# Weight tiles loaded through GpSimd's queue in a four-mixer encoder trunk

## The chip, the core and the metric

The kernel runs on one core of a Trainium2 chip. Its engines each have an instruction stream of their own: PE (TensorE, the matmuls), DVE (VectorE), ACT (ScalarE), POOL (GpSimd) and SP (SyncE). Transfers between HBM and the on-chip memory are issued by SP, ACT or POOL, each in the order of its stream. The metric is the device time in microseconds (us); less is better.

## The reference

Input is `x`, 1 × 512 × 1024 in float32, and the model has two layers. Each layer is a hybrid block of four parallel mixers, then a feed-forward part:

```python
h = RMSNorm(x)
P = h @ W_in          # columns shared out among four mixers and four gates
A: Mamba-2 SSD        B: sparse attention with top-k keys ("dsa")
C: RWKV-7             D: S5 diagonal state space model per 16-channel group
m = sum_n sigmoid(gate_n(h)) * (y_n @ W_branch_n);  x = x + m @ W_out
x = x + SwiGLU(RMSNorm(x))
```

A final RMSNorm follows the second layer. All is float32.

## The kernel before

**Projections.** Activations stand transposed: 1024 features are 8 blocks of 128 partitions, 512 tokens are the free dimension. Every weight matrix is cut into tiles of 128 output columns (`raw`: 128 partitions × 8 blocks × 128 columns, 512 KB). A float32 product is made of three matmuls in a faster format: weights are split into a high part `wh` and a rest `wl`, activations into `hh` and `hl`, and `mm3` (lines 299 to 301) does wh·hh, wh·hl and wl·hh. With 8 blocks a tile takes 24 matmuls of 128 × 512.

**The weight pipeline** is `wload` (line 282): a transfer fills `raw` (line 291, `RAW` = 2 buffers), ACT casts it to `wh` (line 292, 2 buffers), DVE subtracts to give `wl` (line 293, 2 buffers). There are 336 weight tiles in 338 transfers (two tiles come in two pieces). A buffer of `raw` is free when the subtraction of its tile has ended.

**The mixers.** In each layer come S5 (in two halves of 16 groups), dsa, RWKV (two halves) and SSD. Their small operations have long chains on DVE and ACT; projections for the gates (`fill`) stand between them so that PE has work. After them come the merge of the branches, the output projection and the feed-forward, dense series of weight tiles. During the feed-forward of layer 0, the S5 tables of layer 1 are made ahead and put by in HBM.

In the S5 half (`s5`), `s5kt` and `s5pt` are small matmuls on a table `s5E` made by DVE; a result goes to HBM (`ktd`) and comes back as eight pieces into `s5T` (line 1010), over a memset (line 1008). `s5px` is the first matmul series of the half, its result goes twice through a swap of partition halves by transfers (`s5xs`, lines 1004 and 1005) with DVE work between, and `s5py` (lines 1028 and 1029) needs `s5T` and the end of that chain.

At the start, `xtp` (line 218) are transposes of the input, `rbp` (line 185) is a matmul on two small loads, `oh` and `rb`, that prepares the attention's bias, and `colp` (line 442) transposes parameter columns.

**The order.** A scheduler sets each engine's order from priorities (`at("w")` gives weight loads the highest but one) and from times that it estimates. So a change of one operation's engine also moves others.

**Queues.** `q(c)` picks the issuing engine of a transfer by its class from `QUEUE`; a class that isn't there goes to SP. POOL (`"p"`) has the S5 parameters (`sp`, into `s5raw`), `ktd` and `s5T` (`kt`), and the attention's `bias` (`bi`, 8 a layer); some POOL transfers are written out (`oh`, `rb`, `rel`, `dsk`, `dsq`, the S5 tables' way to HBM and back). POOL also does memsets: `mask` (line 617), `s5T`, `NZ` (line 1193, RWKV) and `sdS` (line 1411, SSD).

Of the kernel before, what the change touches and what calls it, by code (L numbers as in the profile page):

```python
# [61 lines left out]
RAW = 2  # L62
FILL = (22, 4, 6)
AH = (2, 8, 11)
QUEUE = {"sp": "p", "qk": "a", "lc": "a", "sv": "a", "kt": "p", "bi": "p"}
FSLOT = ["A0", "A1", "A2", "A3"]
HSLOT = ["A0", "A1", "A2", "A3", "A4", "A5", "B0", "B1", "B2", "B3", "B4"]

# [17 lines left out]
class Trunk:  # L86
# [15 lines left out]
    def q(self, c):  # L102
        return {"a": self.nc.scalar, "p": self.nc.gpsimd, "s": self.nc.sync}[QUEUE.get(c, "s")]

# [177 lines left out]
    def wload(self, pieces, KT, M):  # L282
        nc = self.nc
        n = KT * M
        with self.at("w"):
            raw = self.wp.tile([128, 1024], F32, name="raw", bufs=RAW)
            wh = self.wp.tile([128, 1024], F32R, name="wh")
            wl = self.wp.tile([128, 1024], F32R, name="wl")
            r3 = raw[:, :n].rearrange("p (k m) -> p k m", m=M)
            for m0, src in pieces:  # L290
                nc.sync.dma_start(r3[:, :, m0:m0 + src.shape[1]], src.rearrange("(k p) m -> p k m", p=128))
            nc.scalar.copy(wh[:, :n], raw[:, :n])  # L292
            nc.vector.tensor_sub(wl[:, :n], raw[:, :n], wh[:, :n].bitcast(F32))  # L293
        f = lambda t: t[:, :n].rearrange("p (k m) -> p k m", m=M)
        return f(wh), f(wl)
# [1215 lines left out]
```

## Time and profile before

| what | value |
|---|---|
| time, median of 3 runs | 2346.5 us (2345.83 to 2346.74) |
| time of the profiled execution | 2347.53 us |
| its span, first to last instruction | 2345.7 us |
| PE busy | 2284.1 us, 97% |
| DVE busy | 1435.8 us, 61% |
| ACT busy | 902.8 us, 38% |
| POOL busy | 103.6 us, 4% |
| mean granted clock of PE | 0.988 of full speed |

The profiled execution's time is the span and 1.8 us around it. An engine's busy time leaves out the instructions that issue transfers, so POOL's 4% has no issues in it. The granted clock is 1.00 at 2.4 GHz and 0.50 at 1.2 GHz.

### The profile page before, as it was taken

What the parts mean: (1) busy time and instruction counts of PE and PEld (TensorE: products, weight loads), DVE (VectorE), ACT (ScalarE), POOL (GpSimd) and SP (SyncE); (2) the same over time, 40 slices, a digit from 0 to 9 for tenths busy, and PEclk for the clock granted to TensorE, in tenths of its full rate; (3) what the DMA queues carried; (4) which work ended last, traced back from release to release, by engine and by line L of the source; (5) the groups of instructions that cost most, each with busy time, mean ns of one, the idle gap of its engine ahead of it and who ended that gap; (6) DMA issues with size and microseconds to landing.
All of it is one profiled execution on the core that took longest, in us unless ns stands there. A gap on an engine that the chain in (4) does not pass through costs nothing.

```text
span 2345.7 us, 31925 instructions
## 1 busy us (share of the span) xinstructions
PE 2284.1 (97%) x12348; PEld 1829.7 (78%) x12348; DVE 1435.8 (61%) x2680; ACT 902.8 (38%) x1455; POOL 103.6 (4%) x180
## 2 busy tenths in 40 slices
PE   6999999999999999999999999999999999999998
PEld 5787767877778888887878777677777888888786
DVE  6669767856678597543343695668566775444433
ACT  5343454333552343322232335533346333222223
POOL 3320000000000101000011000000000000000000
PEclk9999999999999999999998999999999999999999
DMA  7545453334166435433365554434242653333232
GB/s 217 123 116 156 123 170 88 108 94 130 37 205 213 118 90 164 129 99 104 117 182 139 131 153 136 134 94 114 76 126 95 207 171 91 99 99 99 86 99 86
DMA packets 421679, 294.17 MB, mean 125 GB/s; under 512 B 56624, under 2 KB 378240, under 8 KB 419928
## 3 DMA queue, kind: packets, MB, share of 16 engines
q1 hardware_dynamic: 412016, 265.58, 38.9%
q0 software_dynamic: 8512, 26.43, 4.1%
q8 instruction: 97, 1.59, 0.3%
q14 instruction: 54, 0.44, 0.1%
q10 hardware_dynamic: 1000, 0.13, 0.0%
HBM read 237.27 MB, written 51.40 MB: 123 GB/s over the span
## 4 chain that ended last, share of the span: by engine, by line
PE 87%; DVE 8%; DMA 2%; issue 2%; ACT 1%; SPq 0%; DVEq 0%; ACTq 0%
PE pj L300 17%; PE pj L301 17%; PE pj L299 17%; PE pf L301 3%; PE pf L300 3%; PE pf L299 3%; PE pb L300 3%; PE pb L301 3%; PE pb L299 3%; DVE wl L293 2%; PE ptp L671 1%; PE lgp L653 1%; PE rwP L1253 1%; PE rwA L1174 1%; PE po L676 1%
## 5 line engine op out<-in xcount | busy, mean ns | idle before, releaser
L299 PE MATMUL pj<-hh,wh 128*128 128x512 f32 x1888 | 751.1, 398 | 5.8 <-DVE conv L1365 2.0
L300 PE MATMUL pj<-hl,wh 128*128 128x512 f32 x1888 | 750.7, 398 | 0.1
L301 PE MATMUL pj<-hh,wl 128*128 128x512 f32 x1888 | 747.3, 396 | 0.9 <-DVE wl L293 0.9
L292 ACT CAST wh<-raw 128x1024 fp32r<-128x1024 f32 x336 | 348.8, 1038 | 946.9 <-PE pj L300 378.0
L293 DVE TENSOR_TENSOR wl<-raw,wh 128x1024 fp32r<-128x1024 f32 x336 | 405.1, 1206 | 373.9 <-ACT wh L292 372.9
L299 PEld LDWEIGHTS pj<-hh,wh 128*128 128x128 f32 x1888 | 356.4, 189 | 89.9 <-issue 9.1
L300 PEld LDWEIGHTS pj<-hl,wh 128*128 128x128 f32 x1888 | 356.3, 189 | 79.6 <-issue 5.8
L301 PEld LDWEIGHTS pj<-hh,wl 128*128 128x128 f32 x1888 | 356.1, 189 | 79.5 <-issue 3.9
L299 PE MATMUL pf<-hid,wh 128*128 128x512 f32 x352 | 137.9, 392 | 1.6 <-ACT wh L292 1.6
L301 PE MATMUL pf<-hid,wl 128*128 128x512 f32 x352 | 137.7, 392 | 0.5 <-DVE wl L293 0.5
L300 PE MATMUL pf<-hid,wh 128*128 128x512 f32 x352 | 137.0, 390 | 0.0
L301 PE MATMUL pb<-yh,wl 128*128 128x512 f32 x256 | 101.1, 395 | 0.0
L300 PE MATMUL pb<-yl,wh 128*128 128x512 f32 x256 | 101.1, 395 | 0.0
L299 PE MATMUL pb<-yh,wh 128*128 128x512 f32 x256 | 100.6, 393 | 0.0
L533 DVE TENSOR_TENSOR fa<-fa,pj 128x512 f32<-128x512 f32 x44 | 30.2, 687 | 95.1 <-PE pj L301 95.0
L530 DVE TENSOR_TENSOR fa<-pj,rb 128x512 f32<-128x512 f32 x44 | 30.4, 690 | 88.5 <-PE pj L301 88.5
L299 PEld LDWEIGHTS pf<-hid,wh 128*128 128x128 f32 x352 | 66.1, 188 | 16.9 <-ACT wh L292 3.4
L301 PEld LDWEIGHTS pf<-hid,wl 128*128 128x128 f32 x352 | 66.1, 188 | 15.9 <-DVE wl L293 2.6
L300 PEld LDWEIGHTS pf<-hid,wh 128*128 128x128 f32 x352 | 66.1, 188 | 13.5
L661 ACT ACTIVATE lg<-lg,mn 128x128 f32<-128x128 f32 (+3 forms) x64 | 35.8, 559 | 62.4 <-DVE mn L659 56.0
L658 DVE TENSOR_TENSOR lg<-lgp,bias 128x128 f32<-128x128 f32 (+3 forms) x64 | 30.8, 486 | 43.1 <-PE lgp L653 42.9
L301 PEld LDWEIGHTS pb<-yh,wl 128*128 128x128 f32 x256 | 48.1, 188 | 10.8 <-issue 0.8
(481 smaller groups left out, 3051.1 us busy)
## 6 DMA issues: line engine op xcount, KB each, us to landing
raw<-in_w_in SPq DMA_DIRECT2D x146, 512.0 KB
raw<-in_ffn_w SPq DMA_DIRECT2D x120, 512.0 KB
gates<-gate SPq DMA_DIRECT2D x64, 256.0 KB
gld<-gates SPq DMA_DIRECT2D x64, 256.0 KB
raw<-in_w_branch SPq DMA_DIRECT2D x32, 512.0 KB
raw<-in_w_out SPq DMA_DIRECT2D x16, 512.0 KB
raw<-in_ffn_w SPq DMA_DIRECT2D x16, 384.0 KB
s5xs<-s5UX SPq DMA_DIRECT2D x16, 256.0 KB
```

The lines of the kernel that those rows point to most:

```text
L292: nc.scalar.copy(wh[:, :n], raw[:, :n])
L293: nc.vector.tensor_sub(wl[:, :n], raw[:, :n], wh[:, :n].bitcast(F32))
L299: mm(ps, wh, ah, start=first, stop=False)
L300: mm(ps, wh, al, start=False, stop=False)
L301: mm(ps, wl, ah, start=False, stop=last)
L530: nc.vector.tensor_mul(a, p1, rb)
L533: nc.vector.tensor_mul(a, a, p3)
L653: i = mm(ps[e][:, :W], q[er[e], qt * 128:(qt + 1) * 128], k[er[e], :W], start=True, stop=True)
L658: nc.vector.tensor_add(t[:, :W], ps[e][:, :W], bias[e][:, 384 - 128 * qt:512])
L661: nc.scalar.activation(t[:, :W], t[:, :W], AF.Exp, scale=-1.0, bias=mn[e][:, qt:qt + 1], accum_out=sm[e][:, qt:qt + 1])
L671: nc.tensor.transpose(pp[:, b * 128:(b + 1) * 128], t[:, b * 128:(b + 1) * 128], self.ident)
L676: i = mm(po[er[e], qt * 128:(qt + 1) * 128], vt[:, b, er[e]], pt[:, e, b * 128:(b + 1) * 128], start=(b == 0), stop=(b == qt))
```

## The change

Weight transfers get a class `"w"`, which `QUEUE` sends to POOL:

```diff
-QUEUE = {"sp": "p", "qk": "a", "lc": "a", "sv": "a", "kt": "p", "bi": "p"}
+QUEUE = {"sp": "p", "qk": "a", "lc": "a", "sv": "a", "kt": "p", "bi": "p", "w": "p"}
...
             for m0, src in pieces:
-                nc.sync.dma_start(r3[:, :, m0:m0 + src.shape[1]], src.rearrange("(k p) m -> p k m", p=128))
+                self.q("w").dma_start(r3[:, :, m0:m0 + src.shape[1]], src.rearrange("(k p) m -> p k m", p=128))
```

All 338 transfers move from SP's stream to POOL's. In the dense series PE, ACT and DVE keep their order; among the mixers and at the start the scheduler orders them anew.

POOL's stream at the start, before, from the last S5 parameter on (`oh`, `rb`, `rel`: loads and stores for the attention's bias; `sm`: a constant):

```order
L761 DMA s5raw<-in_s_c_im 128x4x64
L181 DMA oh<-in_onehot 32x512
L182 DMA oh_224<-in_onehot 32x128
L183 DMA rb<-in_rel_bias 32x8
L173 MEMSET sm_99 128x512
L174 MEMSET sm_99 128x8
L617 MEMSET mask 128x128
L618 MEMSET mask 64x64
L191 DMA rel<-oh 8x512
```

The same place after the change:

```order
L761 DMA s5raw<-in_s_c_im 128x4x64
L291 DMA raw<-in_w_in 128x8x128 x2
L617 MEMSET mask 128x128
L181 DMA oh<-in_onehot 32x512
L618 MEMSET mask 64x64
L182 DMA oh_224<-in_onehot 32x128
L183 DMA rb<-in_rel_bias 32x8
L173 MEMSET sm_99 128x512
L174 MEMSET sm_99 128x8
L291 DMA raw<-in_w_in 128x8x128 x2
```

The first two weight loads come in ahead, and `mask` has moved in front of the loads `oh` and `rb`.

PE's stream at the start, before, from the last transposes of the input to `rbp` (`pj` is the sum of the first weight tile):

```order
L218 MATMUL xtp<-cst,xsB_108 128x128
L299 MATMUL pj<-hh,wh 128x512
L300 MATMUL pj<-hl,wh 128x512
L301 MATMUL pj<-hh,wl 128x512
L299 MATMUL pj<-hh,wh 128x512
L185 MATMUL rbp<-oh,rb 8x512
L187 MATMUL rbp_231<-oh_224,rb 8x128
L300 MATMUL pj<-hl,wh 128x512
```

And after; here these are the first weight matmuls of the program, while before three rows of this kind stand further up between the transposes:

```order
L218 MATMUL xtp<-cst,xsB_108 128x128
L299 MATMUL pj<-hh,wh 128x512
L300 MATMUL pj<-hl,wh 128x512
L299 MATMUL pj<-hh,wh 128x512
L300 MATMUL pj<-hl,wh 128x512
L185 MATMUL rbp<-oh,rb 8x512
L187 MATMUL rbp_231<-oh_224,rb 8x128
L228 MATMUL xrp<-cst,xin_79 128x128
```

Fewer weight matmuls stand ahead of `rbp`, and those with `wl` have moved behind it.

POOL's stream in the first S5 half of layer 0, after the change (the pieces of `s5T`; before, the eight stand in a row with nothing between):

```order
L1010 DMA s5T<-ktd 16x2048
L291 DMA raw<-in_w_in 128x8x128
L1010 DMA s5T<-ktd 16x16x112
L291 DMA raw<-in_w_in 128x8x128
L1010 DMA s5T<-ktd 16x16x96
L291 DMA raw<-in_w_in 128x8x128
L1010 DMA s5T<-ktd 16x16x80
L291 DMA raw<-in_w_in 128x8x128
L1010 DMA s5T<-ktd 16x16x64
L291 DMA raw<-in_w_in 128x8x128
L1010 DMA s5T<-ktd 16x16x48
L1010 DMA s5T<-ktd 16x16x32
```

Five weight loads have come between the pieces; the last three pieces stand behind the fifth.

## Rows read from the trace of the kernel before

**Rows 1.** Page: the span and the busy time of each engine.

```profile
span 2345.7 us, 31925 instructions
PE 2284.1 (97%) x12348; PEld 1829.7 (78%) x12348; DVE 1435.8 (61%) x2680; ACT 902.8 (38%) x1455; POOL 103.6 (4%) x180
```

**Rows 2.** Timeline, steady feed-forward: start, duration, engine, line, operation, [idle before, releaser].

```profile
1022.05 1.06 ACT L292 CAST wh<-raw 128x1024 fp32r<-128x1024 f32 x1 [3.87 <-issue]
...
1027.49 1.05 ACT L292 CAST wh<-raw 128x1024 fp32r<-128x1024 f32 x1 [3.86 <-issue]
...
1023.14 1.23 DVE L293 TENSOR_TENSOR wl<-raw,wh 128x1024 fp32r<-128x1024 f32 x1 [0.21 <-ACT wh L292]
...
1024.39 5.80 SPq L291 DMA_DIRECT2D raw<-in_ffn_w  x2
```

**Rows 3.** Windows: length, PE, PEld, DVE, ACT, POOL busy, PEclk, DMA share, GB/s.

```profile
1027.00:1027.50 0.50, 0.50 (x4) 0.40 (x3) 0.00 (x0) 0.01 (x1) 0.00 (x0) 1.00 0.97 293
1027.50:1028.00 0.50, 0.50 (x4) 0.42 (x3) 0.33 (x1) 0.50 (x1) 0.00 (x0) 1.00 0.11 31
```

**Rows 4.** Transfers: issuing queue, count, KB each, median us from issue to landing.

```profile
raw<-in_ffn_w SPq DMA_DIRECT2D x120, 512.0 KB
...
raw<-in_w_branch SPq DMA_DIRECT2D x32, 512.0 KB
raw<-in_w_out SPq DMA_DIRECT2D x16, 512.0 KB
raw<-in_ffn_w SPq DMA_DIRECT2D x16, 384.0 KB
...
bias<-relb POOLq DMA_DIRECT2D x16, 256.0 KB, 3.4
...
s5raw<-in_s_b_im POOLq DMA_DIRECT2D x4, 128.0 KB, 7.5
...
s5T<-ktd POOLq DMA_DIRECT2D x4, 80.0 KB, 4.6
```

**Rows 5.** Timeline, issues on POOL: eight pieces in one row, and one load form twice.

```profile
11.80 1.21 POOL L761 DMA_DIRECT2D s5raw<-in_s_c_re  x1
...
151.80 4.40 POOL L1010 DMA_DIRECT2D s5T<-ktd  x8 [1.84 <-DMA ktd<-kts]
...
814.52 0.75 POOL L761 DMA_DIRECT2D s5raw<-in_s_c_im  x1
```

**Rows 6.** Timeline, the start: POOL's issues and memset, then PE.

```profile
13.74 1.15 POOL L761 DMA_DIRECT2D s5raw<-in_s_c_im  x1
...
23.89 0.20 POOL L617 MEMSET mask<- 128x128 f32 x1 [5.23 <-PE xtp L218]
...
22.48 0.44 PE L218 MATMUL xtp<-cst,xsA 128*128 128x128 f32 x2 [0.83 <-DVE hl L322]
...
24.90 1.02 PE L185 MATMUL rbp<-oh,rb 32*8 32x512 f32 x2
...
63.45 0.40 PE L900 MATMUL s5kt<-s5tab,s5E 128*128 128x16 f32 x2 [2.64 <-DVE s5E L884]
```

**Rows 7.** Timeline, RWKV in layer 0: a POOL memset, an SP load and its cast.

```profile
509.03 0.15 POOL L1193 MEMSET NZ<- 64x32 f32 x1 [80.79 <-ACT rwPe L1257]
...
494.92 0.38 SPq L291 DMA_DIRECT2D raw<-in_w_in  x1
...
525.27 1.05 ACT L292 CAST wh<-raw 128x1024 fp32r<-128x1024 f32 x1 [3.13 <-PE pj L300]
```

**Rows 8.** Timeline of PE in layer 1's S5, and windows behind its two waits.

```profile
1276.17 0.43 PE L1029 MATMUL s5py<-s5xs,s5O 128*128 128x64 f32 x2 [2.51 <-DVE s5xs L1022]
...
1400.68 0.43 PE L1029 MATMUL s5py<-s5xs,s5O 128*128 128x64 f32 x2 [1.37 <-DVE s5xs L1022]
...
1276.00:1292.00 16.00, 15.83 (x72) 15.16 (x73) 2.48 (x3) 1.17 (x2) 3.42 (x4) 0.57 0.37 116
1403.00:1415.00 12.00, 12.00 (x54) 11.31 (x53) 6.65 (x14) 1.17 (x2) 0.00 (x0) 0.57 0.19 55
```

## The prediction

> **What bounds the kernel now.** I read the busy times first. TensorE works 2284.1 of 2345.7 us [rows 1], so a change pays only where it removes or makes an idle stretch of PE or a stretch at a lower granted clock. Next I read the timeline of a steady stage, the feed-forward block, to see how late a weight may be [rows 2]. ACT casts one weight tile every 1027.49 − 1022.05 = 5.44 us, which is the time of PE's 24 matmuls for a tile (0.227 us each). DVE's subtraction follows the cast and ends at 1023.14 + 1.23 = 1024.37. It gives `raw` free, and SP issues the next load at 1024.39. That row holds two issues, the second a tile later, so the bytes of the first end where the DMA share falls from 0.97 to 0.11, at about 1027.5 [rows 3]: 3.1 us from issue to landing on SP's queue.
>
> That load fills the buffer of the tile after next, so its cast falls at 1022.05 + 2 × 5.44 = 1032.93, **8.5 us** after the issue. PE begins on a tile when the next tile is cast, that is 5.44 us after its own cast (cast of 1022.05: from 1027.49). Cast and subtraction take 1.05 + 1.23 us, so a cast may be another **3.2 us** late before PE waits. A load therefore has 11.7 us from issue to landing before the path sees it.
>
> **The change part by part.**
>
> *338 issues leave SP and enter POOL's queue.* An issue on SP takes 0.38 us [rows 7], and nothing of PE waits on that. On POOL the nearest rows are the small loads: 0.55 us each for eight pieces (4.40 / 8), 0.75 and 1.21 us for a piece of 128 KB [rows 5]. 338 × 0.55 to 1.21 makes 186 to 409 us, on an engine that is busy for 103.6 us of 2345.7 [rows 1]. In the steady stage that is at most 1.2 us in each 5.44. Cost 0; the cover is POOL's emptiness, and without it nothing is lost until an issue nears 5.44 us.
>
> *The landing.* No row shows a 512 KB weight through POOL. By size the nearest POOL transfers are 256 KB in 3.4 us and 128 KB, with smaller pieces and many others in flight, in 7.5 us [rows 4]. I take 7.5, the upper, since a weight tile also has small pieces: 7.5 < 8.5, so even the cast is on time. Cost 0. The lower end costs 0 too.
>
> The issue of the same load form takes 1.21 us at 11.80, where DVE and ACT are loaded, and 0.75 us at 814.52 [rows 5]: a stretch of 0.46 us. The Trainium skill ("SBUF — State Buffer", section "SBUF: two separate sides") says that a DMA issued from GpSimd starves for descriptors while VectorE runs an fp32 copy at its fast rate, 620 ns alone against about 3100 ns overlapped. The trace shows a fifth of that, in the issue. By the skill's figures a landing would be an estimated 7.5 + 2.5 = 10.0 us, still under 11.7, so the sum would be the same, but the margin is the thinner for it.
>
> *Waits of POOL that now hold loads.* POOL's queue is in order, and its fills wait long for a buffer. The longest with loads behind it is the `NZ` memset: it waits 80.8 us and runs at 509.03 [rows 7]. The load wanted at 494.92 stands behind it, but the cast of that load comes at 525.27: held by 14.1 us it still has 525.27 − 509.03 = 16.2 us, against 7.5 + 1.2. I compared the other holds (`bias`, `s5raw`, `sdS`, `mask`) in the same way from the new order; none is longer than 14 us where tiles are slow, or than a few us where they are dense. Cost 0.
>
> *The start.* The first two loads move from 5.87 us on SP to behind 17 POOL transfers, whose last ends its issue at 13.74 + 1.15 = 14.9 [rows 6]. PE's first weight matmul stood inside the transposes; in the new order it stands behind all of them, with four weight matmuls ahead of the `rbp` matmul instead of seven. The two loads of `rbp` (`oh`, `rb`) now stand behind the `mask` memset, which runs at 23.89 when the transposes are over. With up to 1.5 us gained, as three weight matmuls (3 × 0.23) and the 0.83 us wait for `hl` are no longer in between [rows 6], the memset runs at 22.4 to 23.9. Two memsets (0.20 each) and two issues (0.55 to 0.93, taken as 0.6) lead to `rb`'s issue at 24.0 to 25.7; landing after the 3.4 us of [rows 4] is at 27.4 to 29.1. PE got to `rbp` at 24.90, and the order takes it there no later. So a new wait of 2.5 to 4.2 us stands there, with the weight loads partly inside it. Given back: the 0.83 us wait among the transposes, and some of the 2.64 us wait before `s5kt` [rows 6], whose chain on DVE starts earlier in the new order (`colp` stands 20 matmuls earlier on PE), while `s5kt` itself stands 22 matmuls (5.0 us) earlier. Bounds: 2.5 − 0.83 − 2.64 = −1.0, and 4.2 + 0.8 for a chain that gives nothing back = +5.0. I take **+1.5**, near the middle.
>
> *The pieces of `s5T`.* Between its eight pieces stand five weight loads now, and each waits for `raw`. In layer 0, first half, the last three pieces stand behind the 16th load, which is free to go when PE has done 11.4 tiles; `s5py` comes after 12.8 tiles by the new order: 1.4 × 5.44 = 7.6 us. The issue of the load and of three pieces (4 × 0.55 at best, 4 × 1.21 at worst [rows 5]) and the last landing (3.4 to 4.6 [rows 4]) make 5.6 to 9.4 us: from 2.0 us of room to a wait of 1.8 us. Two other halves have about as little room. Together 0 to 5.4; three of the four issues are of the piece form whose row says 0.55, so the sum stays near 7.2, and I take **+0.5** for what company of the two kinds may add.
>
> *SP without the loads.* `s5xs` swaps and `ud`, `zd` transfers no longer stand behind loads that wait for `raw`. That makes only idle engines earlier, since PE waits little on the S5 chain. In layer 1 two waits are worth attention: 2.51 us at 1276.17 and 1.37 us at 1400.68, each followed by a stretch with a mean granted clock of 0.57, between full and the half level of 1.2 GHz: (1 − 0.57) × 16 = 6.9 us and (1 − 0.57) × 12 = 5.2 us lost [rows 8]. The new order has 90 tile matmuls instead of 87 between `s5px` and the first `s5py` in one half and about as much work as before in the other: 3 × 0.227 = 0.7 us of cover. From −0.7 to −16.0; I take **−0.7**, as the wait then still is 1.8 us.
>
> Sum against the profiled execution: its time is 2347.5 (span 2345.7 and 1.8 around it), + 1.5 + 0.5 − 0.7 = 2348.8. That execution lies 1.0 above the median of the runs, 2346.5, so the median after should be 2347.8: **2348 us**. A difference of 0.2% (4.7 us) is about what a measurement of this kernel can tell from no change.
>
> The Trainium skill ("DMA: Bandwidth & Descriptors", section "Issuing engines are not separate DMA queues") says that transfers of all issuers end on the same 16 engines and that another issuer saves only issue time. The trace agrees that issue time is all there is to save (0.38 us of SP, hidden), which is the forecast above.
>
> **The rivals.**
> - *The `s5T` pieces come late (slower).* If a piece behind a weight load lands over 8 us after that load is issued, PE waits at `s5py` in up to three halves, each 1 to 2 us, and the clock falls behind it as after 1276 and 1400, 5.2 to 6.9 us each: 3 × 1.5 + 6.9 + 5.2 = 16.6, or 2365; with one or two, 2354 to 2360. For it: the margin is half a microsecond. Against: the piece form's own rows give 7.2 us. Chance 0.24.
> - *Layer 1's S5 waits go (faster).* If the freed SP queue and the other order of DVE's work bring the chain 2.5 us forward, both waits and both slow-clock stretches vanish: 2.51 + 6.9 + 1.37 + 5.2 = 16.0, so 2332; one of them gives 2338 to 2341. For it: the swaps lose their neighbours. Against: the chain's last step is DVE work, not a transfer. Chance 0.27.
> - *Loads starve PE (slower by much).* If issue to landing passes 11.7 us in the dense stages, each us over costs up to 1 us on each of their 184 loads: 1 us over gives about 2530. The rows stop at 7.5. The starving that the Trainium skill describes under the same title would lead here at twice its figure. Chance 0.08.
> - *Nothing of it matters*: the move saves hidden issue time and all moved waits stay covered: 2346 to 2347. It lies inside my own range.
>
> **How the numbers follow.** The forecast has 0.41, its own range 2344 to 2353 from the bounds of the start (−1.0 to +5.0) and of the pieces; 0.03 of it lies past 2351.2, where no change ends. So faster 0.27, same 0.38, and slower 0.24 + 0.08 + 0.03 = 0.35. The range leaves out starvation and the tails of the other two: 2331 to 2366.
>
> **What would show it.** Right: PE's waits on `wh` and `wl` stay under 2 us in sum, ACT's casts in the feed-forward keep their 5.44 us, POOL is busy some 290 to 510 us if its issues are added, and a new wait of 2.5 to 4.2 us stands at `rbp`. Wrong: PE waiting for `s5T` at `s5py`, waits of ACT's cast on `raw` in the dense stages, or the granted clock at 1.00 right after layer 1's `s5py`.

## Result and the profile after

The changed kernel takes 2368.0 us in the median (2365.3 to 2371.8), before 2346.6: ratio 1.0094, 95% interval 1.0078 to 1.0111. It is **slower by 22 us**, 0.9%. The predicted 2348, and the range up to 2366, were too low.

The page of the changed kernel, its profiled execution (2370.0 us), gives the span, the busy times and two groups of weight loads (busy time and mean ns of one issue, then the idle time ahead of them):

```profile
span 2368.2 us, 32004 instructions
PE 2304.2 (97%) x12348; PEld 1840.7 (78%) x12348; DVE 1439.7 (61%) x2680; ACT 901.3 (38%) x1453; POOL 399.4 (17%) x518
...
L291 POOL DMA_DIRECT2D raw<-in_w_in x150 | 134.2, 895 | 908.8 <-DVE wl L293 626.6
L291 POOL DMA_DIRECT2D raw<-in_ffn_w x136 | 120.4, 885 | 594.5 <-DVE wl L293 501.5
...
raw<-in_w_in POOLq DMA_DIRECT2D x146, 512.0 KB, 4.5
raw<-in_ffn_w POOLq DMA_DIRECT2D x120, 512.0 KB, 4.4
```

Of 22.5 us more span than in [rows 1], PE is busy in 2304.2 − 2284.1 = 20.1 us and idle in 2.4 us. PE does the same 12348 instructions, so 20 us are the same work done slower. The loads themselves look well: an issue takes 0.89 us and a load lands in 4.5 us, where 8.5 us are to be had [rows 2].

The chain of the feed-forward is untouched. ACT casts every 5.43 us, 5.44 in [rows 2], and POOL issues a load each time DVE gives a buffer free; the timeline of both in the changed kernel:

```profile
1030.28 1.05 ACT L292 CAST wh<-raw 128x1024 fp32r<-128x1024 f32 x1 [3.87 <-PE pj L300]
...
1035.71 1.05 ACT L292 CAST wh<-raw 128x1024 fp32r<-128x1024 f32 x1 [3.86 <-PE pj L300]
...
1032.88 0.88 POOL L291 DMA_DIRECT2D raw<-in_ffn_w  x1 [4.56 <-DVE wl L293]
```

The slower work stands in RWKV. Its time lost to the clock is (1 − granted clock) × length of each stretch. Windows of the changed kernel over its six slow stretches there (columns as in [rows 3]; the granted clock is the third number from the end):

```profile
448.00:454.00 6.00, 5.87 (x30) 4.87 (x31) 4.85 (x13) 1.71 (x3) 0.72 (x1) 0.72 0.22 76
486.00:498.00 12.00, 12.00 (x92) 9.05 (x88) 3.98 (x5) 4.76 (x10) 0.88 (x1) 0.57 0.30 78
574.00:584.00 10.00, 10.00 (x113) 7.78 (x112) 3.38 (x4) 4.45 (x7) 0.89 (x1) 0.66 0.31 89
1640.00:1644.00 4.00, 4.00 (x12) 3.12 (x11) 3.54 (x7) 1.63 (x2) 0.88 (x1) 0.57 0.96 202
1650.00:1672.00 22.00, 22.00 (x169) 17.29 (x167) 6.53 (x11) 5.36 (x11) 0.88 (x1) 0.53 0.24 67
1746.00:1754.00 8.00, 8.00 (x95) 6.61 (x93) 2.35 (x3) 3.00 (x5) 0.87 (x1) 0.57 0.20 62
```

The kernel before has three there, the second with a wait of 2.0 us in it:

```profile
484.00:490.00 6.00, 6.00 (x54) 4.70 (x52) 1.24 (x2) 0.58 (x1) 0.00 (x0) 0.72 0.74 211
562.00:568.00 6.00, 5.00 (x15) 4.01 (x16) 4.14 (x6) 3.11 (x4) 0.00 (x0) 0.72 0.89 209
1644.00:1650.00 6.00, 6.00 (x47) 4.77 (x46) 1.99 (x3) 0.57 (x1) 0.00 (x0) 0.72 0.89 252
```

The losses sum to 1.7 + 5.2 + 3.4 + 1.7 + 10.3 + 3.4 = 25.7 us after and 3 × 1.7 = 5.0 us before: **20.7 us**, as much as PE's busy time grew. (Outside RWKV, 5.2 us less in layer 1's S5 stand against three stretches more of 1.7 us each.) PE has no idle time in the two long ones (12.00 of 12.00, 22.00 of 22.00), so a list of waits does not show them.

PE's list of waits in the changed kernel (us in sum, times, longest):

```profile
PE ptp L671 <- DVE lg L668: 9.0, 22, 0.9
PE kkn L1146 <- ACT rwprep L1143: 3.9, 4, 1.1
PE zx L1212 <- DMA zts<-zt: 3.5, 2, 1.8
...
PE pj L299 <- ACT wh L292: 2.7, 2, 2.5
PE s5py L1029 <- DVE s5xs L1022: 2.7, 1, 2.7
```

PE never waits for `s5T`. `kkn` (a small matmul series of RWKV that wants ACT) waited 2.6 us in sum before, and `zx` for a z transfer not at all. The second S5 wait of layer 1 [rows 8] is gone, with its slow stretch; the first and its stretch stay:

```profile
1276.00:1292.00 16.00, 14.06 (x65) 13.67 (x66) 3.12 (x3) 1.17 (x2) 3.23 (x3) 0.58 0.31 100
1400.00:1420.00 20.00, 19.73 (x101) 14.46 (x96) 19.83 (x44) 9.12 (x16) 2.65 (x3) 1.00 0.47 153
```

What has changed in RWKV is PE's order. `rwA`, `zx`, `zz` are small matmuls (32 to 128 columns a piece); the z stage is the inversion in the middle of RWKV's first half. Before, in program order, from the last `rwA` of this stage:

```order
L1174 MATMUL rwA<-AR,BK 128x128 x11
L1212 MATMUL zx<-zts,M_3164 32x32 x16
L1174 MATMUL rwA<-AR,BK 128x128 x5
L301 MATMUL pj<-hh,wl 128x512
L1217 MATMUL zz<-M_3164,zts 32x32 x16
L299 MATMUL pj<-hh,wh 128x512
...
L1212 MATMUL zx<-zts,M_3165 32x32 x16
```

The dots are 12 projection matmuls. After:

```order
L1212 MATMUL zx<-zts,M_3164 32x32 x16
L328 MATMUL bon<-rkl,bd_r 128x512
L1174 MATMUL rwA<-AR,BK 128x128 x5
L1217 MATMUL zz<-M_3164,zts 32x32 x16
L1174 MATMUL rwA<-AR,BK 128x128 x2
L1212 MATMUL zx<-zts,M_3165 32x32 x16
L1174 MATMUL rwA<-AR,BK 128x128 x8
L299 MATMUL pj<-hh,wh 128x512
```

Here 65 matmuls stand in one row with no projection matmul among them, and only five follow before the next `zz`. The likely reason: the z transfers no longer share SP's queue with weight loads, and the scheduler, which orders by times that it estimates, has put the z stage forward in PE's stream.

### The profile page after: what moved, and what is told of

Read it like the earlier page. It is cut to its first block, busy times and chain, and to the rows that moved or that the text cites. A ratio compares the mean times of both kernels' runs of the same rounds, so it can differ in the third digit from the quotient of the medians.

```text
span 2368.2 us, 32004 instructions
## 1 busy us (share of the span) xinstructions
PE 2304.2 (97%) x12348; PEld 1840.7 (78%) x12348; DVE 1439.7 (61%) x2680; ACT 901.3 (38%) x1453; POOL 399.4 (17%) x518
## 3 DMA queue, kind: packets, MB, share of 16 engines
q1 hardware_dynamic: 83024, 92.18, 12.4%
## 4 chain that ended last, share of the span: by engine, by line
PE 84%; DVE 8%; DMA 4%; issue 2%; ACT 1%; SPq 0%; POOL 0%; ACTq 0%; DVEq 0%; POOLq 0%
PE pj L300 16%; PE pj L299 16%; PE pj L301 16%; PE pf L301 3%; PE pf L300 3%; PE pf L299 3%; PE pb L299 2%; PE pb L301 2%; PE pb L300 2%; DVE wl L293 2%; PE rwA L1174 1%; PE rwP L1253 1%; PE lgp L653 1%; PE ptp L671 1%; PE rwP L1281 1%
## 5 line engine op out<-in xcount | busy, mean ns | idle before, releaser
L291 POOL DMA_DIRECT2D raw<-in_w_in x150 | 134.2, 895 | 908.8 <-DVE wl L293 626.6
L291 POOL DMA_DIRECT2D raw<-in_ffn_w x136 | 120.4, 885 | 594.5 <-DVE wl L293 501.5
L301 PEld LDWEIGHTS pf<-hid,wl 128*128 128x128 f32 x352 | 66.1, 188 | 15.9 <-DVE wl L293 2.6
```

Source lines behind the costliest of these rows:

```text
L291: self.q("w").dma_start(r3[:, :, m0:m0 + src.shape[1]], src.rearrange("(k p) m -> p k m", p=128))
L301: mm(ps, wl, ah, start=False, stop=last)
```

## Experiments

Two theories stood at first. **Order**: the new PE order costs the time, by the granted clock; the loads are innocent. **Queue**: loads through POOL cost it. To hold an order, some kernels get edges between PE's (or also DVE's and ACT's) instructions, which fix which is issued first and add no wait:

```python
for a, b in zip(order, order[1:]):     # order: numbers of the engine's instructions
    tc.add_manual_dep(mine[b], mine[a].name, NoSync)
```

Each ratio is to the kernel before, run beside it on the same chip; its median lay between 2343.8 and 2346.6 us. So what a version keeps of the 22 us, or gives back, is read from the ratios.

**e1: old order, loads through POOL.**

```diff
 # the changed kernel, and:
+    pin(tc, {"PE": order of before, "DVE": order of before, "Activation": order of before})
```

> All 338 weight loads go through POOL, but PE, DVE and ACT keep the order of the kernel before, instruction by instruction (edges that fix the order, no waits). Order theory: the 22 us come from the new order alone, so this is within 0.2% of before, 2342 to 2351 us, with seven or eight stretches at a granted clock under 1 as before (28 to 30 us lost in sum). Queue theory: loads through POOL cost the time, so this is near the changed kernel, 2362 to 2372 us.

2364.5 us, ratio 1.0094 (1.0078 to 1.0111). The order theory alone fails: the lost clock is near that of before, but PE waits. Its timeline, a line of DVE's, and the two windows behind:

```profile
119.93 1.08 PE L1028 MATMUL s5py<-s5UX,s5T 128*128 128x64 f32 x4 [7.49 <-DMA s5T<-ktd]
...
204.77 0.29 DVE L658 TENSOR_TENSOR lg<-lgp,bias 128x128 f32<-128x128 f32 x1 [7.53 <-DMA bias<-relb]
...
114.00:128.00 14.00, 8.07 (x27) 6.81 (x28) 1.26 (x2) 1.01 (x2) 7.71 (x16) 0.63 0.59 139
204.00:216.00 12.00, 6.99 (x20) 5.54 (x21) 9.49 (x30) 2.68 (x8) 0.91 (x1) 0.57 0.22 71
```

The last pieces of `s5T` stood behind this load, which waited 3.19 us for its buffer, on POOL:

```profile
113.28 0.90 POOL L291 DMA_DIRECT2D raw<-in_w_in  x1 [3.19 <-DVE wl L293]
114.17 1.68 POOL L1010 DMA_DIRECT2D s5T<-ktd  x3
```

So the in-order queue does hold small transfers behind loads, and in the old order that costs 7.5 us at `s5py` and up to 8.7 us at `ptp` behind `bias`, and 0.37 × 14 + 0.43 × 12 = 10.3 us of clock. The changed kernel does not wait there: in its order some 120 projection matmuls, not 57, stand between `s5px` and `s5py` in this half.

**e2: new order, loads on SP** (the kernel before, the three engines held to the changed kernel's order).

> The loads stay in SP's queue, but PE, DVE and ACT are held to the order of the changed kernel. Order theory: 2362 to 2374 us, since the small RWKV matmuls stand together and the granted clock falls after them (about 50 us lost in sum); a little more than the changed kernel if SP's in-order queue makes PE wait for transfers behind loads. Queue theory: near before, 2344 to 2352 us.

2433.4 us, 1.0385 (1.0365 to 1.0406): worse than either theory said. PE waited 15.9 us at `s5px` for `ud` transfers and 9.1 at `zx`, whose transfers share SP's queue with the loads, and the slow stretches of the whole kernel grew to 84 us lost, from 46 in the changed one. The new order fits only the new queue; the run doesn't separate the theories.

**e3: RWKV in the old order, loads through POOL.** The edges cover only the PE instructions of the two RWKV stages.

> Loads through POOL as in the change; only in the two RWKV stages the PE instructions are held to the order of before, all else is free. If the RWKV order is the cause, the losses at 448, 486, 574, 1640, 1650 and 1746 us (1.7 + 5.1 + 3.4 + 1.7 + 10.2 + 3.4 of the changed kernel, against 1.7 + 1.7 + 1.7 before) go for the most part: 2368 - 20 = 2348, range 2343 to 2355. If the losses are spread over all stages or come from the transfers, it stays above 2360.

2353.1 us, 1.0045 (1.0032 to 1.0059): within its range, and by the ratios 11 to 12 of the 22 us are gone, with loads through POOL as before it. In its profiled execution, the lowest of its five, PE's busy time is back at that of before (2284.1):

```profile
PE 2284.9 (97%) x12348; PEld 1826.3 (78%) x12348; DVE 1438.3 (61%) x2680; ACT 902.8 (38%) x1455; POOL 399.1 (17%) x518
```

Its span is 4.7 us over that of before, nearly all of it idle time.

**e4: dense series alone.**

```diff
 # the kernel before, and:
-QUEUE = {... "kt": "p", "bi": "p"}
+QUEUE = {... "kt": "p", "bi": "p", "wd": "p"}
...
-                nc.sync.dma_start(...
+                self.q("wd" if self.dense else "w").dma_start(...
```

> Only the 184 loads of the dense series (branch merge, output projection, feed-forward) go through POOL; the 154 of the mixers stay on SP, and PE's order is that of before but for a few rows. Order theory: as before, 2342 to 2351 us. Queue theory (each load through POOL costs its share): 2347 + 22 x 184 / 338 = 2359 us.

Here `"wd"` is POOL and `"w"`, a class that isn't in `QUEUE`, is SP. 2345.3 us, 1.0003 (0.9992 to 1.0015): 184 loads through POOL cost nothing that shows. The queue theory falls for these.

**e5 and e6: POOL for loads alone.** ktd, `s5T` and `bias` go to SP, in e5 with the old order, in e6 free.

```diff
-QUEUE = {"sp": "p", "qk": "a", "lc": "a", "sv": "a", "kt": "p", "bi": "p", "w": "p"}
+QUEUE = {"sp": "p", "qk": "a", "lc": "a", "sv": "a", "w": "p"}
```

> As e1 (all weight loads through POOL, PE, DVE and ACT in the order of before), but the pieces of s5T with ktd, and the attention's bias, go through SP instead of POOL, so that nothing small stands behind a weight load that waits for its buffer. Theory of the shared in-order queue: the 7.5 us wait for s5T, the 8.7 us wait behind bias and the two slow-clock stretches after them (5.1 us each) go: 2364.5 - 26 = 2339 to 2348. If the issue through POOL itself is what costs, it stays at 2360 to 2366.

> The changed kernel, free order, with the s5T pieces, ktd and bias on SP. The row of 65 small RWKV matmuls without a projection matmul between (before: at most 40 in these stages) stays in this order. Theory of order: the RWKV clock losses stay, 2358 to 2370. If the shared queue is the cause in the changed kernel too: 2343 to 2350.

2389.3 (1.0172, 1.0152 to 1.0192) and 2387.5 (1.0166, 1.0137 to 1.0196): both misses. The `s5T` wait went, but DVE's list of waits has `bias` late nine times in e5:

```profile
DVE lg L658 <- DMA bias<-relb: 38.8, 9, 8.1
```

SP's own queue waits too (374.8 us in sum for gates before their stores, in this run), so `bias` only came to stand behind something else. At the longest of these waits, SP issues it right behind the eight pieces of `s5T`:

```profile
189.18 4.94 SPq L1010 DMA_DIRECT2D s5T<-ktd  x8
194.35 0.41 SPq L645 DMA_DIRECT2D bias<-relb  x1
```

In e6 `bias` is late four times (12.4 us), and PE waits 23.6 us at `ptp`, 9.0 in the changed kernel, and 8.2 at `zx`.

**e10: only `s5T` off the queue** (ktd and `s5T` on SP, `bias` on POOL, old order).

> As e1 (loads through POOL, old order), but ktd and the pieces of s5T go through SP; bias stays on POOL. Shared-queue theory: the 7.5 us wait at s5py and the slow-clock stretch after it (5.1 us) go and the wait behind bias stays: 2364.5 - 12.6 = 2352, range 2347 to 2357. If the hold behind weight loads is not what made the pieces late: 2360 to 2368.

2353.5 us, 1.0039 (1.0023 to 1.0055), near the 2352 that the hold theory said. The first window of e1 is whole, as forecast. But so is the second, whose wait for `bias` was to stay, and a new wait stands in layer 1:

```profile
114.00:128.00 14.00, 13.84 (x71) 11.45 (x70) 10.46 (x10) 4.97 (x7) 1.77 (x2) 1.00 0.51 150
204.00:216.00 12.00, 11.78 (x59) 8.46 (x58) 11.75 (x33) 4.33 (x8) 0.88 (x1) 1.00 0.34 106
...
1389.71 0.47 PE L671 MATMUL ptp<-cst,lg 128*128 128x128 f32 x1 [4.64 <-DVE lg L668]
```

With `ktd` and `s5T` off POOL, `bias` is first issued there at 172.7 us instead of 198.3. Behind the new wait 3.4 us of clock are lost, and `s5py` waits 4.4 us at 1277.68 (3.1 in e1). So the hold of `s5T` is shown by the window; that the time came out near the forecast is luck.

**e7: z stage of the first half in the old order.**

> The changed kernel, but some 150 PE instructions in each layer, those around the inversion of the first RWKV half (rwA, zx, zz and the projection matmuls between), are held to the order of before; all else is free. If the row of small matmuls is what lowers the granted clock, the stretches at 486 and 1650 us (5.1 and 10.2 us lost) fall to the 1.7 us of before each: 2368 - 12 = 2356, range 2351 to 2360. If not: 2364 to 2372.

2356.2 us, 1.0041 (1.0027 to 1.0055), the forecast to the microsecond. In its profile the stretches at 490 and 1654 us lose 3.4 and 1.7 us. Some 300 instructions of PE's stream hold 12 of the 22 us, as much as all of RWKV in e3.

**e8: z transfers on POOL too.**

```diff
-QUEUE = {... "bi": "p", "w": "p"}
+QUEUE = {... "bi": "p", "w": "p", "z": "p"}
```

> The changed kernel, but the z transfers of RWKV go through POOL too, so that they stand between weight loads again, as they did in SP's queue before; in the order that comes out the row of 65 small matmuls is gone. Order theory: about 2356 as e7, range 2348 to 2362; a wait of PE at zx for a z transfer held behind loads could add up to 5. If the clock losses come from elsewhere: 2364 to 2376.

2365.4 us, 1.0084 (1.007 to 1.0098), a miss. The z stage is mended (1.7 and 3.4 us lost), but waits stand elsewhere (4.4 us at `pb` for ACT, 4.5 at `kkn`, 3.5 at `zx`): the scheduler ordered all anew.

**e9, e12, e13: the row put into the kernel before.** Loads on SP; in each layer 14, 21 and 7 projection matmuls are moved ahead of the small ones.

```diff
+T T T T T T T T T T T T T T
 rwA x11, zx x16, rwA x5
-T
 zz x16
-T T T T T T T T T T T T T
 zx x16
```

> The kernel before, loads on SP, all engines in the old order, but in each layer 14 projection matmuls of the z stage of RWKV's first half are moved ahead of the small matmuls that they stood between (rwA, zx, zz, zx), so that 64 small matmuls stand in one row; nothing is added or taken away. If such a row lowers the granted clock, the stretches at 484 and 1644 us (1.7 us lost each) grow to 3.4 to 8.5 each, as at 486 and 1650 in the changed kernel: 2350 to 2359 us. If the row is harmless and the loss came with the transfers: 2344 to 2349.

> As e9, but 21 projection matmuls instead of 14 are moved ahead of the small ones, so that behind the row of 64 only five stand before the next zz and the chunk's small matmuls, as in the changed kernel. If what lowers the clock is a long stretch with few projection matmuls, not the row itself, the z stage now loses 3.4 to 8.5 us in each layer: 2350 to 2359 us. If the order of the small matmuls does nothing at all: 2344 to 2349, and the loss in the changed kernel has to come with what else its z stage has (the 1.1 us wait at kkn).

> As e12 without the row: only seven projection matmuls are moved ahead, so that five stand between the second zx and the next zz, and the 14 between the first small ones stay. Stretch theory: less of the loss than e12, 2346 to 2353. If the order does nothing: 2344 to 2349.

2344.8 (1.000, 0.9986 to 1.0014), 2345.6 (1.000, 0.9979 to 1.002) and 2343.7 (0.9992, 0.9978 to 1.0006). My theory that the row by itself lowers the clock, or a thin stage, falls: the intervals end at +0.2% or below. That rests on the medians. The profiled execution of e12 is the fastest of its twelve (2338 to 2358 us), that of e9 the second of its twelve, so they don't show what the slower ones have. Windows of e12 over the row in both layers:

```profile
482.00:498.00 16.00, 16.00 (x216) 13.02 (x215) 6.62 (x11) 5.74 (x12) 0.00 (x0) 1.00 0.61 168
1640.00:1656.00 16.00, 16.00 (x194) 12.67 (x192) 5.71 (x10) 5.85 (x15) 0.00 (x0) 1.00 0.37 97
```

**e11: start and RWKV old.** As e3 with the first 330 matmuls held too.

> As e3 (changed kernel, RWKV's PE order of before) with the first 330 matmuls of the program also in the order of before. Order theory: the 2.9 us wait for the first weight and its slow-clock stretch (3.4 us) at the start go: 2353 - 6 = 2347, range 2343 to 2351. If the start's losses come from the transfers that stand behind POOL's parameter loads, they stay: 2351 to 2355.

2351.1 us, 1.0028 (1.0012 to 1.0043): at the upper edge of its range, and 2 us under e3 (4 by the ratios), less than the runs of either spread. Inconclusive.

**e14, e15, e16: PE's waits out of the changed order.** e14 is the changed order itself, e15 moves each `kkn` series behind eight projection matmuls, e16 also the first `zx` of the second half.

```diff
-kkn x8
 T T T T T T T T
+kkn x8
```

> The changed kernel itself, its PE order written out and fixed; every engine's order is that of the changed kernel. It shows how far the time of that order spreads on this chip beside the others of this call: 2362 to 2372 us.

> The changed kernel's PE order with the eight small kkn matmuls of each of the eight groups moved behind the next eight projection matmuls (1.8 us later), so that PE no longer waits there for ACT (3.9 us in four waits before, 1.14 at most). If a wait of about 1.1 us is what lowers the clock, the stretches after 448 and 1640 (1.7 each) and most of those at 486 and 1650 (5.1 and 10.2) go too: 2368 - 4 - 10 = 2354, range 2348 to 2360. If only the waits themselves count: 2364. If PE waits as long later: 2368.

> As e15, and the first zx matmuls of the second half (1.8 and 1.7 us wait for a z transfer) are moved behind eight more projection matmuls. Wait theory: their waits (3.5) and the stretches after them (3.4 each) go on top of e15: 10 us less than e15, 2344, range 2340 to 2352. If waits do not set the clock: 3.5 us less than e15 at most.

2363.7 (1.0092, 1.0074 to 1.0109), 2372.4 (1.0127, 1.0106 to 1.0148) and 2374.9 (1.0128, 1.0114 to 1.0142). The waits at `kkn` went, in e16 those at `zx` too, and no time came back. Part of the gain went into new waits: in e15 and e16 PE waits 5.7 us in six times at `bon`, for ACT. In e16 layer 0's stretch lost 3.4 us, 8.5 in e14, but those of the second half lost more (5.1 and 6.8). But the last of them ahead of layer 1's z stage stands some 25 us ahead of the stretch, and the stretch is there in all three, so the theory that it takes a wait of PE close ahead of it falls too. Windows of e14 and e15, and that wait in e15:

```profile
1646.00:1668.00 22.00, 22.00 (x169) 17.28 (x167) 6.58 (x11) 5.37 (x11) 0.88 (x1) 0.53 0.24 67
...
1652.00:1674.00 22.00, 22.00 (x168) 17.36 (x168) 6.74 (x11) 5.37 (x11) 0.88 (x1) 0.53 0.23 67
...
1626.15 0.50 PE L327 MATMUL bon<-rkh,bd_r 128*128 128x512 f32 x1 [1.34 <-ACT rkh L318]
```

**e17 and e18: the place of the row.** In e9 and e12 the row came later, since projection matmuls stood ahead of it. e17 has the changed kernel's layout in the kernel before, e18 the late row in the changed kernel.

```diff
 # e17, loads on SP            # e18, loads on POOL
 kkn, 24 T                      kkn, 24 T
-6 T, (14 T among the small)   +21 T
 64 small, 5 T                  65 small, 5 T, chunk work
-7 T                           -21 T (of 27, at the end of the half)
+27 T (at the end of the half)
```

> The kernel before, loads on SP, with the z stage laid out as in the changed kernel: 24 projection matmuls after kkn, then the 64 small ones in one row, then five; 27 projection matmuls (6.1 us) that stood in this stage come at the end of the half instead. So the row comes 6 us sooner after kkn than in e9 and e12. Order theory: it loses 8.5 and 10.2 us at the granted clock as the changed order does (e14) and is 12 to 17 us slower than before, 2357 to 2364 us, and up to 5 more if PE waits for a z transfer. If the loss needs POOL's loads: 2344 to 2350.

> The changed kernel's order with 21 projection matmuls from the end of the half moved ahead of the row of 65 small ones, as in e12; the row itself and all that follows it stay as they are. Order theory, with the row's place after kkn deciding: the stretches at 486 and 1650 (8.5 and 10.2 us in e14) go, 2364 - 17 = 2347, range 2345 to 2354. If the loss comes with POOL's loads and not with the place of the row: 2361 to 2370.

e17: 2356.8 us, 1.0045 (1.0028 to 1.0063). The z stage loses 0.43 × 16 = 6.9 us in each layer, where the kernel of the other order of the same instructions loses 1.7:

```profile
484.00:500.00 16.00, 16.00 (x134) 11.96 (x131) 4.20 (x8) 5.37 (x11) 0.00 (x0) 0.57 0.34 91
1648.00:1664.00 16.00, 16.00 (x129) 11.89 (x127) 4.10 (x8) 5.37 (x11) 0.00 (x0) 0.57 0.35 91
```

No load goes through POOL here (its busy time in these windows is 0.00), and PE waits for no z transfer. So **the order alone makes a loss in the z stage**, 6.9 us in each layer, less than the 10.3 of the changed kernel's layer 1. What comes with it is a short wait of PE at the head of the row, 5 us ahead of the stretch in each layer, that neither the kernel before nor e12 has:

```profile
479.21 0.37 PE L1174 MATMUL rwA<-AR,BK 64*128 64x128 f32 x1 [0.70 <-DVE BK L1165]
...
1643.05 0.37 PE L1174 MATMUL rwA<-AR,BK 64*128 64x128 f32 x1 [0.70 <-DVE BK L1165]
```

No run separates the two. e18: 2371.5 us, 1.0108 (1.0088 to 1.0127), a miss. Layer 1's stretch shrank (3.4 us), layer 0's did not (8.5). Where projection matmuls were taken from the end of the half, PE has a new wait, 9.6 us at `gnt` for DVE in two times, and a slow stretch of 3.4 us lost begins at each. It doesn't settle the place of the row.

None of the versions is faster than before beyond its interval; the dense loads can go either way.

## Why the prediction was wrong, point by point

- *338 issues on POOL, cost 0*: right. 0.89 us each against 0.55 to 1.21; POOL busy 399 us against 290 to 510. e4 shows it for the dense series.
- *Landing 7.5 us, cost 0*: right in cost; it is 3.9 to 4.5. The starving of which the Trainium skill ("SBUF — State Buffer", section "SBUF: two separate sides") warns does not show: no estimated 10.0 us landing in the profile's medians. It had little room to: the warning is of copies, and DVE's `COPY` rows make 25 us of its 1439.7, so no run here tests it.
- *Waits of POOL that hold loads, cost 0*: right for the changed kernel, whose list of PE's waits names weights for 2.7 us (2.5 of them at the start) and 1.8 us at one `wl`, where DVE's S5 work ran ahead of the subtraction. The sign that went with it, under 2 us in sum on `wh` and `wl`, could not have held: with 2.1 us in the feed-forward it is 6.6, and it was 3.0 before.
- *The start, +1.5*: right in size, wrong in place. No wait stands at `rbp`, which PE reaches at 24.93; 2.5 us stand at the first weight matmul, at 23.32, and 0.2 behind it. Less 0.83, 0.84 (of the `s5kt` wait [rows 6]) and 1.9 (a wait for ACT at `xrp` that is gone), and with 1.1 more behind `us` and 1.7 us of clock at 26 to 30, it is +1.9. The size is luck: the term has neither the last two waits nor the clock. (Its 25.7 for `rb`'s issue should be 25.5.)
- *`s5T` pieces, +0.5*: 0. The mechanism of the slower rival is real, as e1 and e10 show, 7.5 us and 5.2 us of clock, but only in the old order; the new one gave `s5py` more room. The time came out near that rival's 2365 by another way, which is luck. (With a late piece in all three halves, 5.4, the forecast's own range would end at 2356, not 2353.)
- *Layer 1's S5, −0.7*: −6.4, by half of the faster rival. The 1.37 us wait and its 5.2 us are gone; the first wait is 2.68 us and stays with its stretch. No run isolates what took the second away; in e1, with the old order and the loads on POOL, 1.17 us of it are left.
- *"That makes only idle engines earlier, since PE waits little on the S5 chain"*: **this step failed.** I had read the new order of RWKV only for whether transfers and weights come in time, and priced it at nothing. It cost 20.7 us of granted clock, and 1.3 us more at `kkn` and 3.5 at `zx`. [rows 8] had shown that PE can lose time while busy; I used that only where the order changed a wait.

The terms make 1.9 − 6.4 + 20.7 + 4.8 = 21.0 of the 22.5 us of span. With 1.7 + 1.7 us of clock at 1264 and 1872, 2.8 us more of waits (`ptp`, `wl`, `rwl`) and 3.7 less (two for `conv`) it is 23.5, within 1 us.

That PE's order in one stage of RWKV costs some 12 of the 22 us is shown from both sides: taken out of the changed kernel (e7: −12; with the rest of RWKV, e3: −11), put into the kernel before (e17: +11). That RWKV accounts for nearly all of PE's longer busy time is read from single profiles (20.7 us of clock against 20.1 us of busy time in the changed kernel; in e3 the busy time is back at that of before). What in that order lowers the clock **stays open**. A row of 64 small matmuls is not enough (e9), nor a thin stage behind it (e12), nor is a PE wait within the 25 us ahead needed (e15, e16), though in e17 one stands there. The layout that loses in e17 is e12's with 27 projection matmuls moved from ahead of the row to the end of the half, so that the row comes 6 us sooner after `kkn`; in the changed kernel, putting 21 of them back mended one layer of two (e18). Open as well are the 9 to 11 us that e3, and the 5 to 7 us that e11, keep over before.

## What to carry to other kernels

Moving a transfer to another queue also moves everything that a scheduler orders by estimated landing times; compare the new compute order stage by stage before pricing the transfer, also where no engine will wait. Look at the granted clock of stretches in which PE is busy without a gap: a list of waits is blind to them, and here they make up nearly all of the 20 us by which PE's busy time grew. In a shared in-order queue, a small transfer that is wanted soon must not stand behind a load that waits for its buffer (7.5 us at `s5T`); moving it to another queue helps only if nothing waits there either (`s5T` yes, `bias` no).

## What the runs showed of the hardware that was not expected

- The granted clock went to 0.53 over 22 us in which PE was busy without a gap (1650 to 1672 us), and in e17 to 0.57 over 16 us, while e12, with the same small matmuls in a row, kept 1.00 in its fastest execution.
- A weight load of 512 KB takes POOL 0.89 us to issue and lands in 4.5 us, not longer than a 128 KB load of the S5 parameters (6.0 us for `s5raw` in the same run).
- Executions of one PE order differ in which of the slow stretches they have. The changed kernel's profiled execution lost 5.2 us at 486 and 3.4 at 574; that of e14, with the same order, lost 8.5 at 486 and none at 574. The 12 runs of e9 lie between 2338 and 2352 us; differences under some 5 us between single profiles say little here.
